# Steps of the gated weights set apart, four more H and L tiles, and the residual on VectorE

## The chip, the cores and the metric

The kernel runs on one core of a Trainium2 chip. The metric is the device time of one execution in microseconds, measured in several runs. One more execution was taken with the hardware profiler; all rows of the trace are from it, and its times count from the first instruction of the span.

## The reference

One encoder block for 256 tokens of width 2048, in float32. A first part (gated spatial mixing, neighbourhood attention, output projection and a LayerNorm) makes `x1`; then a retrieval over 16384 single-neuron experts follows, and a second LayerNorm:

```python
q = (xf @ wq).reshape(T, PEER_HEADS, 2, PEER_QHALF)
s = einsum('thpk,hpnk->thpn', q, subkeys)
top_s, top_i = top_k(s, 16)               # per head and half, then 16 of the 256 sums
gate = softmax(best_s)                    # 8 heads x 16 experts a token
h = einsum('td,tkd->tk', xb, u_tab[ib])   # experts' inputs
w = gb * gelu(h)
y = einsum('tk,tkd->td', w, v_tab[ib])
x = layernorm(alpha * x1 + y)
```

## The kernel before, in words

Every large product runs in three passes of a number split in two: `H` is the operand rounded to the matmul's format (ScalarE, L135), `L` is the rest (VectorE, L136). A *unit* is one 128x512 piece of streamed operand: `emit_split` writes its H and L into tiles of the pool `hlp`, and later the unit's matmuls read them. `hlp` has LOOK + 1 = 4 pairs. `run_units` writes the program in order: for each unit it first emits the splits that may run ahead (at most two in a turn, as long as four pairs or fewer are out), then the unit's matmuls, then what a finished block asks for (`posts`), then one step of each background *lane* (attention, top-k, list making, the residual, the final normalization). Every engine executes its own instructions in that order.

The stages that the change touches:

- *Retrieval.* 64 units of the query weights; top-k runs on VectorE in the background, `VEC_PER_UNIT` = 0.72 us a unit. From here on the new pool of the change exists.
- *Expert products.* All 128 blocks of experts are multiplied densely, four units a block (`stationary_units`: per unit four pairs of matmuls, L224 of 512 columns and L226 of 256). Blocks alternate between two PSUM banks. After a block ScalarE copies one half of the sums (L268), VectorE adds the other (L613), and ScalarE makes the Gelu (L620) and writes it to a table in device memory (L622). SyncE loads the weights into five `raw` tiles of two units each. Lists of the tokens' experts are made meanwhile.
- *Lists ready.* SyncE is given four loads of value blocks `vraw` (L761) and six of table tiles `tb` (L772); the last raw loads stand behind them.
- *Values.* `SEQ` is a list of 109 blocks of 128 value rows: 53 serve both halves of the tokens (24 matmuls) and 56 one half (12). A block has four units (dc 0 to 3, 512 columns each) of three matmuls a half: L235, L236, L237. Its rows come by a gather on GpSimd (L763, five `vraw` tiles), its gates and activations by gathers from the table (L775, four `tb` tiles). `w_split` makes the stationary operand: product of gate and activation (VectorE, L786), its high half (ScalarE, L787), its low half (VectorE, L788), all just before the split of the block's first unit; then it issues the gather for three blocks later.
- *Residual.* After four blocks, `residual` loads `x1` (`x1d`) and the LayerNorm's two rows by GpSimd's queue and makes 16 operations of 128x512 on GpSimd (L1060), six units apart.
- *End.* The three last blocks (LAST) run column part by column part; their H and L tiles are kept, since the second half of the tokens is multiplied after the first while VectorE finishes the first half.

The lines of the splits in the code:

```python
act.activation(H, raw, AF.Copy)
vec.tensor_tensor(L, raw, H.bitcast(F32), op=OP.subtract)
```

Of the kernel before, what the change touches and what calls it, by code (L numbers as in the profile page):

```python
# [31 lines left out]

RAW_BUFS = 5
LOOK = 3

# [25 lines left out]
def tile_encoder_block(ctx: ExitStack, tc: tile.TileContext, a, out):  # L63
# [55 lines left out]
    def emit_split():  # L119
        n = state["split"]  # L120
        if n >= len(units):
            return
        if units[n].early:
            units[n].early()
        kind, r, h = units[n].src
        src = vraws if kind else raws
        raw = src[r][0][:, h * 512:(h + 1) * 512]
        if units[n].dest:
            H, L = units[n].dest()
        else:  # L130
            H = hlp.tile([P, 512], F32R, name="H", tag="H")
            L = hlp.tile([P, 512], F32R, name="L", tag="L")
        if len(H.shape) == 3:
            raw = raw.rearrange("p (k t) -> p k t", t=T)
        act.activation(H, raw, AF.Copy)  # L135
        vec.tensor_tensor(L, raw, H.bitcast(F32), op=OP.subtract)  # L136
        HL[n] = (H, L)
        state["split"] += 1
        src[r][1] -= 1
        if src[r][1] == 0:  # L140
            del src[r]
            if kind:
                emit_values()
            else:
                emit_load()

    credit = {"v": 0.0}

    def step_lanes():
# [28 lines left out]
    def run_units(upto):  # L178
        while state["mm"] < upto:
            n = state["mm"]  # L180
            ahead = 0
            while state["split"] < len(units):
                u = units[state["split"]]
                if state["split"] > n and ahead == 2 or not u.dest and state["out"] > LOOK:
                    break
                state["out"] += not u.dest
                ahead += 1
# [202 lines left out]
    def pause(n):  # L390
        for _ in range(n):
            yield
# [383 lines left out]
                if n == DENSE:  # L776
                    after(i, put[tb] + hput[tb])

    def w_split(n):
        def f():  # L780
            hs = SEQ[n][0]
            s = slice(hs[0], hs[-1] + 1)
            t = tabs.pop(n)
            w = vp.tile([P, 2, 2, P], F32R, name="w", tag="wv", bufs=4)
            p = t[:, s, P:]
            vec.tensor_tensor(p, t[:, s, :P], p, op=OP.mult)  # L786
            act.activation(w[:, 0, s, :], p, AF.Copy)  # L787
            vec.tensor_tensor(w[:, 1, s, :], p, w[:, 0, s, :].bitcast(F32), op=OP.subtract)  # L788
            W[n] = w
            while vst["tab"] < min(n + 4, len(SEQ)) and (SEQ[vst["tab"]][1] < 0 or len(hput[1]) == NKEY):  # L790
                emit_tab()
        return f

    def v_units():
        us = []
        places = [(n, dc) for n in range(len(SEQ) - LAST) for dc in range(4)]
        places += [(n, dc) for dc in range(4) for n in range(len(SEQ) - LAST, len(SEQ))]
        seen = set()
        for n, dc in places:
            hs = SEQ[n][0]  # L800

# [5 lines left out]
            def mm(H, L, n=n, dc=dc, hs=hs):  # L807
# [8 lines left out]
                elif hs == (0, 1):  # L816
                    part(1)

            u = Unit(mm, pre=pre, early=None if n in seen else w_split(n),
                     dest=(lambda n=n, dc=dc: [endp.tile([P, 512], F32R, name="%s%d_%d" % (q, n, dc)) for q in "HL"])  # L820
                     if n >= len(SEQ) - LAST else None,
                     post=(lambda dc=dc: fin["y"](dc)) if n == len(SEQ) - 1 else None)
            u.src = (1, n, dc)
            seen.add(n)
            us.append(u)
        return us


# [157 lines left out]

    up_stack = ExitStack()
    upp = up_stack.enter_context(tc.tile_pool(name="upp", bufs=1))
    gate["g"] = upp.tile([P, 2, PH, TK], F32, name="gate_g")
    gate["i"] = upp.tile([P, 2, PH, TK], U32, name="gate_i")  # L990
    for n, dt in (("tab", U32), ("val", U32)):
# [59 lines left out]
    def residual():  # L1051
# [3 lines left out]
        for tb in range(2):  # L1055
            for c in range(4):
                s = slice(c * 512, (c + 1) * 512)
                for j, op in enumerate((OP.mult, OP.add)):
                    yield from pause(6)
                    pool.tensor_tensor(x1b[:, tb, s], x1b[:, tb, s], gb1[:, j, s], op=op)  # L1060
        ys["y"] = gb1

    def y_ready(dc):
# [136 lines left out]
```

## Time and profile before

| | us |
|---|---|
| median of 3 runs | 1761.7 |
| lowest, highest | 1757.7, 1762.09 |
| the profiled execution | 1757.17 |
| its span, first to last instruction | 1755.4 |
| TensorE matmuls busy | 1695.9 (97%) |
| VectorE busy | 1295.6 (74%) |
| ScalarE busy | 947.7 (54%) |
| GpSimd busy | 858.2 (49%) |
| mean granted clock of TensorE | 0.989 |

PE is TensorE, PEld its weight loads, DVE VectorE, ACT ScalarE, POOL GpSimd, SP SyncE; a small q behind an engine's name is its queue issuing. Busy time says how full an engine is over the whole span. It does not say which engine was waited for at a given moment; windows and timelines of a stretch do.

### The profile page before, as it was taken

How to read it: one execution, taken by the hardware profiler on the slowest of the kernel's cores; microseconds unless marked ns; L12 is line 12 of the kernel's file. 1: busy time of each engine (PE TensorE's matmuls, PEld its weight loads, DVE VectorE, ACT ScalarE, POOL GpSimd, SP SyncE). 2: the span in 40 equal slices, each digit the busy share in tenths (PEclk: the TensorE clock that was granted, in tenths of full speed). 3: DMA queues.
4: the chain of work that ended last, by engine and by line, in shares of the span. 5: the costliest groups of instructions: out<-in, count | busy, mean ns of one | idle time of the engine just before them, and what ended most of it. 6: DMA issues, size and time to landing. Idle time of an engine off the chain costs nothing. (4 is left out here: it accounts for less than half of the span.)

```text
span 1755.4 us, 26746 instructions
## 1 busy us (share of the span) xinstructions
PE 1695.9 (97%) x8544; PEld 1375.6 (78%) x8544; DVE 1295.6 (74%) x2835; ACT 947.7 (54%) x1843; POOL 858.2 (49%) x710
## 2 busy tenths in 40 slices
PE   8999999989999999999999999998989999999995
PEld 7888777878888888888888878887866777777774
DVE  5776665677999998555556888885678777777778
ACT  5655555465555555555555445444545555556553
POOL 0000000000688888888886225771367666666662
PEclk9999999999999999999999999999999999999998
DMA  9998543555678888888888996557687788888881
GB/s 344 379 313 271 190 164 138 193 183 200 175 188 198 202 195 200 220 213 203 214 211 254 359 357 212 189 189 279 240 319 260 262 285 290 291 294 287 285 299 65
DMA packets 201043, 421.66 MB, mean 240 GB/s; under 512 B 53586, under 2 KB 120196, under 8 KB 185796
## 3 DMA queue, kind: packets, MB, share of 16 engines
q1 hardware_dynamic: 98660, 247.50, 41.0%
q0 software_dynamic: 64800, 154.60, 31.1%
q10 hardware_dynamic: 37440, 17.84, 3.8%
q8 instruction: 67, 1.10, 0.3%
q14 instruction: 76, 0.62, 0.1%
HBM read 381.97 MB, written 37.88 MB: 239 GB/s over the span
## 5 line engine op out<-in xcount | busy, mean ns | idle before, releaser
L224 PE MATMUL bank<-xHL,H 128*128 128x512 f32 x2688 | 967.7, 402 | 6.8 <-ACT H L135 6.5
L136 DVE TENSOR_TENSOR L<-raw,H 128x512 fp32r<-128x512 f32 x798 | 545.5, 689 | 304.7 <-ACT H L135 297.1
L226 PE MATMUL bank<-xHL,L 128*128 128x256 f32 x2688 | 759.8, 283 | 5.8 <-DVE L L136 5.0
L135 ACT ACTIVATE H<-raw 128x512 fp32r<-128x512 f32 x798 | 488.2, 628 | 439.7 <-PE bank L224 207.1
L224 PEld LDWEIGHTS bank<-xHL,H 128*128 128x128 f32 x2688 | 506.6, 188 | 129.8 <-ACT H L135 10.4
L226 PEld LDWEIGHTS bank<-xHL,L 128*128 128x128 f32 x2688 | 508.7, 189 | 21.3 <-DVE L L136 19.6
L597 POOL DMA_INDIRECT tab<-gate_g,gate_i x256 | 419.0, 1637 | 133.4 <-issue 75.6
L136 DVE TENSOR_TENSOR L<-vraw,H 128x512 fp32r<-128x512 f32 x436 | 293.4, 717 | 67.5 <-ACT H L135 60.3
L135 ACT ACTIVATE H<-vraw 128x512 fp32r<-128x512 f32 x436 | 248.7, 620 | 64.2 <-PE bank L236 62.8
L235 PE MATMUL bank<-H,w 128*128 128x512 f32 x648 | 260.3, 402 | 11.5 <-ACT H L135 11.4
L237 PE MATMUL bank<-L,w 128*128 128x512 f32 x648 | 264.0, 407 | 3.2 <-DVE L L136 2.9
L236 PE MATMUL bank<-H,w 128*128 128x512 f32 x648 | 258.5, 399 | 2.1 <-DVE w L788 2.1
L775 POOL DMA_INDIRECT tb<-tab,list_tab x154 | 182.2, 1183 | 46.1 <-issue 45.5
L982 POOL DMA_DIRECT2D x1d<-res x1 | 0.5, 547 | 381.3 <-DVE res L952 381.3
L763 POOL DMA_INDIRECT vraw<-in_pv,list_val x105 | 99.5, 948 | 162.7 <-DVE L L136 89.1
L237 PEld LDWEIGHTS bank<-L,w 128*128 128x128 f32 x648 | 122.7, 189 | 53.9 <-DVE L L136 27.2
L235 PEld LDWEIGHTS bank<-H,w 128*128 128x128 f32 x648 | 122.8, 190 | 51.6 <-ACT H L135 26.3
L236 PEld LDWEIGHTS bank<-H,w 128*128 128x128 f32 x648 | 122.8, 190 | 30.4 <-DVE w L788 2.7
L707 POOL TENSOR_SCALAR hotA<-iota,w 128x128 bf16<-128x128 bf16 x124 | 92.9, 760 | 61.6 <-PE bank L718 35.3
L787 ACT ACTIVATE w<-tb 128x128 fp32r<-128x128 f32 (+1 forms) x109 | 39.5, 363 | 145.1 <-DVE tb L786 144.0
L620 ACT ACTIVATE hs<-half 128x256 f32<-128x256 f32 x128 | 52.4, 409 | 88.3 <-DVE half L613 88.2
L788 DVE TENSOR_TENSOR w<-tb,w 128x128 fp32r<-128x128 f32 (+1 forms) x109 | 47.7, 438 | 46.8 <-ACT w L787 46.8
(185 smaller groups left out, 1345.3 us busy)
## 6 DMA issues: line engine op xcount, KB each, us to landing
raw<-in_ut SPq DMA_DIRECT2D x256, 512.0 KB
tab<-zero SPq DMA_DIRECT2D x32, 512.0 KB
raw<-in_wqk SPq DMA_DIRECT2D x32, 512.0 KB
raw<-in_wout SPq DMA_DIRECT2D x32, 512.0 KB
raw<-in_wq SPq DMA_DIRECT2D x32, 512.0 KB
tab<-hs ACTq DMA_DIRECT2D x256, 64.0 KB
gc<-tab POOLq DMA_DIRECT2D x32, 512.0 KB
raw<-in_wu SPq DMA_DIRECT2D x16, 512.0 KB
```

Of the source, the lines that this page charges most:

```text
L135: act.activation(H, raw, AF.Copy)
L136: vec.tensor_tensor(L, raw, H.bitcast(F32), op=OP.subtract)
L224: pe.matmul(ps, lhsT=h, rhs=xs["X"][:, k].rearrange("p j t -> p (j t)"), start=k == 0, stop=False)
L226: pe.matmul(ps[:, T:], lhsT=l, rhs=xs["H"][:, k, :], start=False, stop=k == KD - 1)
L235: pe.matmul(ps, lhsT=h, rhs=H, start=first, stop=False)
L236: pe.matmul(ps, lhsT=l, rhs=H, start=False, stop=False)
L237: pe.matmul(ps, lhsT=h, rhs=L, start=False, stop=last)
L597: i = apart(tb, pool.indirect_dma_start(out=tab[tb].rearrange("e (t o) -> (e t) o", o=1), out_offset=bass.IndirectOffsetOnAxis(ap=gate["i" ...
L620: act.activation(s, held["t"], AF.Gelu)
L707: pool.tensor_scalar(A, iota, row[:, b:b + 1], None, op0=OP.is_equal)
L763: pool.indirect_dma_start(out=t, out_offset=None, in_=a["pv"], in_offset=column(n, "val"))
L775: i = pool.indirect_dma_start(out=t[:, tb, :], out_offset=None, in_=tab[tb], in_offset=column(n, "tab")).ins
```

## The change

Three things change together. (1) From the retrieval on there are eight H and L pairs (`MORE` = 4 in a new pool `more`), and splits may run up to seven units ahead. (2) `w_split` becomes `w_steps`: the product stands three units before the block's first split, the high half one before, the low half at it; the gather of the table tile for three blocks later stays with the low half. (3) The residual's 16 operations are VectorE's, 16 units apart. So that memory suffices, the kept tiles of the end use the five raw tiles first.

```diff
+MORE = 4
@@ emit_split
-            H = hlp.tile([P, 512], F32R, name="H", tag="H")
-            L = hlp.tile([P, 512], F32R, name="L", tag="L")
+            p = hlp
+            if more:
+                p = more["p"] if more["n"] > LOOK else hlp
+                more["n"] = (more["n"] + 1) % (LOOK + 1 + MORE)
+            H = p.tile([P, 512], F32R, name="H", tag="H")
+            L = p.tile([P, 512], F32R, name="L", tag="L")
@@ run_units
-                if state["split"] > n and ahead == 2 or not u.dest and state["out"] > LOOK:
+                if state["split"] > n and ahead == 2 or not u.dest and state["out"] > LOOK + (MORE if more else 0):
@@ w_split becomes w_steps
+    def w_steps(n):
+        hs = SEQ[n][0]
+        s = slice(hs[0], hs[-1] + 1)
+        def product():
+            t = tabs[n]
+            vec.tensor_tensor(t[:, s, P:], t[:, s, :P], t[:, s, P:], op=OP.mult)
+        def high():
+            W[n] = vp.tile([P, 2, 2, P], F32R, name="w", tag="wv", bufs=4)
+            act.activation(W[n][:, 0, s, :], tabs[n][:, s, P:], AF.Copy)
+        def low():
+            vec.tensor_tensor(W[n][:, 1, s, :], tabs.pop(n)[:, s, P:], W[n][:, 0, s, :].bitcast(F32), op=OP.subtract)
             while vst["tab"] < min(n + 4, len(SEQ)) and (SEQ[vst["tab"]][1] < 0 or len(hput[1]) == NKEY):
                 emit_tab()
-        return f
+        return product, high, low
@@ v_units
+        def kept(i):
+            if i < RAW_BUFS:
+                t = rawp.tile([P, 1024], F32R, name="raw", tag="raw")
+                return t[:, :512], t[:, 512:]
+            return [endp.tile([P, 512], F32R, name="%s%d" % (q, i)) for q in "HL"]
...
+            if n not in seen:
+                seen.add(n)
+                for back, f in zip((3, 1, 0), w_steps(n)):
+                    todo[max(len(us) - back, 0)].append(f)
@@ after the first LayerNorm
+    more.update(p=up_stack.enter_context(tc.tile_pool(name="more", bufs=MORE)), n=0)
@@ residual
-                    yield from pause(6)
-                    pool.tensor_tensor(x1b[:, tb, s], x1b[:, tb, s], gb1[:, j, s], op=op)
+                    yield from pause(16)
+                    vec.tensor_tensor(x1b[:, tb, s], x1b[:, tb, s], gb1[:, j, s], op=op)
```

The same work stands in another order on the engines. Line numbers of the changed kernel are higher by 5 to 23 (L135 and L136 become L140 and L141, L786 to L788 become L792, L796 and L799); the numbers behind names count tiles and differ between the two.

VectorE in the values' stage, before: `tb` is a table tile and its product, `w` the low half, `L` the splits.

```order
L786 TENSOR_TENSOR tb_14369<-tb_14369 128x2x128
L788 TENSOR_TENSOR w_14519<-tb_14369,w_14519 128x256
L136 TENSOR_TENSOR L_14526<-vraw_14306,H_14525 128x512
L136 TENSOR_TENSOR L_14533<-vraw_14306,H_14532 128x512
L136 TENSOR_TENSOR L_14541<-vraw_14306,H_14540 128x512
L136 TENSOR_TENSOR L_14548<-vraw_14306,H_14547 128x512
L786 TENSOR_TENSOR tb_14418<-tb_14418 128x128
L788 TENSOR_TENSOR w_14559<-tb_14418,w_14559 128x128
```

The same place on VectorE in the changed kernel:

```order
L799 TENSOR_TENSOR w_14487<-tb_14348,w_14487 128x256
L141 TENSOR_TENSOR L_14508<-vraw_14273,H_14507 128x512
L792 TENSOR_TENSOR tb_14397<-tb_14397 128x128
L141 TENSOR_TENSOR L_14519<-vraw_14273,H_14518 128x512
L141 TENSOR_TENSOR L_14529<-vraw_14273,H_14528 128x512
L141 TENSOR_TENSOR L_14541<-vraw_14273,H_14540 128x512
L799 TENSOR_TENSOR w_14538<-tb_14397,w_14538 128x128
L141 TENSOR_TENSOR L_14554<-vraw_14334,H_14553 128x512
```

The product of the next block (`tb_14397`) now stands after the first split of the block at hand, three splits ahead of its low half.

SyncE where the lists are ready, before: the last value block, six table tiles, then the last raw tiles of the expert weights.

```order
L761 DMA vraw_13931<-in_pv 128x2048
L772 DMA tb_13935<-tab0_96 128x256
L772 DMA tb_13935<-tab1_97 128x256
L772 DMA tb_13938<-tab0_96 128x256
L772 DMA tb_13938<-tab1_97 128x256
L772 DMA tb_13941<-tab0_96 128x256
L772 DMA tb_13941<-tab1_97 128x256
L113 DMA raw_13948<-in_ut 128x1024
L113 DMA raw_13982<-in_ut 128x1024
L113 DMA raw_14008<-in_ut 128x1024
L113 DMA raw_14042<-in_ut 128x1024
```

The same place on SyncE in the changed kernel:

```order
L767 DMA vraw_13954<-in_pv 128x2048
L778 DMA tb_13958<-tab0_96 128x256
L778 DMA tb_13958<-tab1_97 128x256
L778 DMA tb_13961<-tab0_96 128x256
L778 DMA tb_13961<-tab1_97 128x256
L778 DMA tb_13964<-tab0_96 128x256
L778 DMA tb_13964<-tab1_97 128x256
L114 DMA raw_13971<-in_ut 128x1024
L114 DMA raw_14005<-in_ut 128x1024
```

Two raw loads instead of four stand behind the table tiles; the other two were issued before.

ScalarE at the end of the expert products, before: `half` is the copy of a block's half-sums, `hs` the Gelu; `raw_13948` is the first of the raw tiles behind the table tiles.

```order
L135 ACTIVATE H_14064<-raw_13894 128x512
L268 ACTIVATE half_14077<-bank0_14010 128x256
L135 ACTIVATE H_14080<-raw_13948 128x512
L620 ACTIVATE hs_14092<-half_14077 128x256
L622 DMA tab0_96<-hs_14092 128x128
L622 DMA tab1_97<-hs_14092 128x128
L135 ACTIVATE H_14096<-raw_13948 128x512
L135 ACTIVATE H_14108<-raw_13982 128x512
L135 ACTIVATE H_14120<-raw_13982 128x512
L268 ACTIVATE half_14133<-bank1_14068 128x256
```

The same in the changed kernel, where `raw_13971` is the first such tile:

```order
L140 ACTIVATE H_14083<-raw_13917 128x512
L274 ACTIVATE half_14096<-bank0_14031 128x256
L140 ACTIVATE H_14099<-raw_13971 128x512
L626 ACTIVATE hs_14111<-half_14096 128x256
L628 DMA tab0_96<-hs_14111 128x128
L628 DMA tab1_97<-hs_14111 128x128
L140 ACTIVATE H_14115<-raw_13971 128x512
L140 ACTIVATE H_14127<-raw_14005 128x512
L140 ACTIVATE H_14139<-raw_14005 128x512
L274 ACTIVATE half_14152<-bank1_14087 128x256
```

The two pieces read alike, but the splits are those of units eight ahead where they were four ahead: in the changed kernel `H_14139` is the last unit of the last block, and `half_14152` belongs to the last block but two, whose bank the last block needs.

## Rows read from the trace of the kernel before

**Rows 1.** Windows in us; busy time (instructions) by engine, PEclk granted clock, DMA share, GB/s.
```profile
450.00:700.00 250.00, 245.25 (x1367) 208.03 (x1367) 232.77 (x732) 136.57 (x266) 211.92 (x126) 1.00 0.83 195
700.00:950.00 250.00, 249.50 (x1412) 215.96 (x1411) 137.97 (x226) 139.89 (x271) 208.51 (x133) 1.00 0.84 210
950.00:1050.00 100.00, 98.21 (x532) 80.88 (x531) 81.48 (x114) 48.10 (x97) 26.85 (x31) 1.00 1.03 358
...
1200.00:1250.00 50.00, 45.27 (x236) 38.12 (x235) 24.91 (x47) 23.75 (x48) 2.98 (x3) 0.93 0.76 280
1250.00:1400.00 150.00, 139.32 (x553) 103.73 (x552) 117.83 (x180) 76.78 (x151) 103.26 (x94) 0.98 0.77 278
1400.00:1700.00 300.00, 296.12 (x1220) 223.15 (x1219) 224.82 (x423) 178.66 (x352) 188.98 (x174) 1.00 0.83 290
```

**Rows 2.** Timeline, TensorE, first value matmuls: start us, us, instruction [idle before <-releaser].
```profile
1241.80 0.39 PE L235 MATMUL bank<-H,w 128*128 128x512 f32 x1
...
1242.50 0.39 PE L235 MATMUL bank<-H,w 128*128 128x512 f32 x1
```

**Rows 3.** Timelines of SyncE (SPq), ScalarE and TensorE where the lists are ready.
```profile
1211.07 12.14 SPq L772 DMA_DIRECT2D tb<-tab  x6
...
1227.25 0.63 ACT L135 ACTIVATE H<-raw 128x512 fp32r<-128x512 f32 x1 [8.77 <-DMA raw<-in_ut]
1227.78 0.40 ACT L620 ACTIVATE hs<-half 128x256 f32<-128x256 f32 x1
1228.21 0.82 ACTq L622 DMA_DIRECT2D tab<-hs  x2
...
1227.93 0.80 PE L224 MATMUL bank<-xHL,H 128*128 128x512 f32 x1 [4.73 <-ACT H L135]
...
1233.48 0.40 PE L224 MATMUL bank<-xHL,H 128*128 128x512 f32 x1
```

**Rows 4.** Timeline, 1268 to 1294: GpSimd, VectorE, TensorE.
```profile
1268.79 1.01 POOL L775 DMA_INDIRECT tb<-tab,list_tab  x1 [0.30 <-issue]
...
1279.47 1.56 POOL L1060 TENSOR_TENSOR yx<-yx 128x512 f32<-128x512 f32 x1 [5.44 <-DMA yx<-in_ln_g]
...
1282.66 0.43 DVE L786 TENSOR_TENSOR tb<-tb 128x256 f32<-128x256 f32 x1 [2.78 <-DMA tb<-tab,list_tab]
...
1284.11 0.50 PE L235 MATMUL bank<-H,w 128*128 128x512 f32 x1 [2.65 <-ACT H L135]
...
1292.20 2.33 DVE L136 TENSOR_TENSOR L<-vraw,H 128x512 fp32r<-128x512 f32 x1 [0.71 <-ACT H L135]
```

**Rows 5.** Groups by line, 1238 to 1400: count | busy us, mean ns | idle before.
```profile
L136 DVE TENSOR_TENSOR L<-vraw,H 128x512 fp32r<-128x512 f32 x128 | 94.4, 781 | 19.0 <-ACT H L135 16.5 <-DMA vraw<-in_pv,list_val 0.7
...
L1060 POOL TENSOR_TENSOR yx<-yx 128x512 f32<-128x512 f32 x16 | 21.0, 1313 | 5.7 <-DMA yx<-in_ln_g 5.4
```

**Rows 6.** The same groups, 1450 to 1650, with the product.
```profile
L136 DVE TENSOR_TENSOR L<-vraw,H 128x512 fp32r<-128x512 f32 x187 | 121.0, 691 | 30.6 <-ACT H L135 27.9 <-DMA tb<-tab,list_tab 0.7
...
L786 DVE TENSOR_TENSOR tb<-tb 128x256 f32<-128x256 f32 x21 | 8.8, 417 | 0.0
```

**Rows 7.** Timeline of all engines at a block's start, 1505 to 1508.
```profile
1505.99 0.42 ACT L787 ACTIVATE w<-tb 128x256 fp32r<-128x256 f32 x1 [1.09 <-DVE tb L786]
...
1506.44 0.42 DVE L788 TENSOR_TENSOR w<-tb,w 128x256 fp32r<-128x256 f32 x1 [0.48 <-ACT w L787]
...
1507.32 0.40 PE L236 MATMUL bank<-H,w 128*128 128x512 f32 x1
...
1507.71 0.50 PE L237 MATMUL bank<-L,w 128*128 128x512 f32 x1
```

**Rows 8.** Timeline, VectorE in the last part.
```profile
1720.90 6.11 DVE L136 TENSOR_TENSOR L<-vraw,H 128x512 fp32r<-128x512 f32 x10
...
1749.92 0.75 DVE L1047 SCALAR_TENSOR_TENSOR yx<-yx,rs,b2r 128x512 f32<-128x512 f32 x1
```

**Rows 9.** Timeline, GpSimd at the start of the retrieval.
```profile
393.61 0.53 POOL L998 DMA_DIRECT2D subT<-in_subT  x1 [8.14 <-DMA x1d<-res]
```

More of the change, by code (lines that the diff above doesn't have):

```diff
@@ L145, in emit_split @@
                 emit_load()
+    more = {}
     credit = {"v": 0.0}
@@ L777, in emit_tab @@
                     after(i, put[tb] + hput[tb])
[L779 to L789, printed above, removed]
+    def w_steps(n):
[9 more added lines that the diff above has]
+            vec.tensor_tensor(W[n][:, 1, s, :], tabs.pop(n)[:, s, P:], W[n][:, 0, s, :].bitcast(F32), op=OP.subtract)
             while vst["tab"] < min(n + 4, len(SEQ)) and (SEQ[vst["tab"]][1] < 0 or len(hput[1]) == NKEY):
                 emit_tab()
-        return f
+        return product, high, low
     def v_units():
@@ L798, in v_units @@
         seen = set()
+        todo = [[] for _ in places]
+        def kept(i):
[3 more added lines that the diff above has]
+            return [endp.tile([P, 512], F32R, name="%s%d" % (q, i)) for q in "HL"]
         for n, dc in places:
@@ L817, in mm @@
                     part(1)
-            u = Unit(mm, pre=pre, early=None if n in seen else w_split(n),
-                     dest=(lambda n=n, dc=dc: [endp.tile([P, 512], F32R, name="%s%d_%d" % (q, n, dc)) for q in "HL"])
-                     if n >= len(SEQ) - LAST else None,
+            u = Unit(mm, pre=pre, dest=(lambda i=len(us) - len(places) + 4 * LAST: kept(i)) if n >= len(SEQ) - LAST else None,
                      post=(lambda dc=dc: fin["y"](dc)) if n == len(SEQ) - 1 else None)
             u.src = (1, n, dc)
-            seen.add(n)
+            if n not in seen:
+                seen.add(n)
+                for back, f in zip((3, 1, 0), w_steps(n)):
+                    todo[max(len(us) - back, 0)].append(f)
             us.append(u)
+        for u, fs in zip(us, todo):
+            u.early = (lambda fs=fs: [f() for f in fs]) if fs else None
         return us
```

## The prediction

> **What bounds the kernel now.** I read the page first: TensorE is busy for 97% of the span, so time can come only from stretches where it waits or runs slowly. The table of windows [rows 1] shows which those are: the number of matmuls in a stretch, times what one needs when nothing holds it, is taken from the stretch's length. In the values' stage three matmuls start in 0.70 us when undisturbed (1241.80 to 1242.50) [rows 2], so one needs 0.2333 us. From 1250 to 1400 there are 553, or 129.0 us: 21.0 us are lost. From 1400 to 1700 there are 1220, or 284.7: 15.3 lost. In the expert products 1412 matmuls, a pair for each 128 of depth, fill 700 to 950 with TensorE nearly always busy [rows 1], 0.354 us a pair and 1.416 a unit of four; I take that as the floor there. From 950 to 1050, 266 pairs need 94.2 us: 5.8 lost.
>
> The timelines then tell who was late. When the lists are ready, SyncE holds 12.14 us at the table tiles, with raw tiles of the expert weights queued behind it; ScalarE waits 8.77 us for such a tile and TensorE 4.73 us [rows 3]. After the gap the matmuls take longer (0.80 for the first, 0.40 again at 1233.48) and the granted clock of the window is 0.93 [rows 1]; eight pairs take the 5.55 us from 1227.93 to 1233.48 where 2.8 would do. That stall costs 4.73 + 2.7 = 7.4 us. In the values' stage GpSimd waits 5.44 us for the residual's loads, with gathers queued behind it, and TensorE then stands for 2.65 us [rows 4]. After that each of 16 GpSimd operations of 1.31 us holds up VectorE [rows 5]. From 1400 on the residual is over and the loss has another shape: at a block's start ScalarE waits 1.09 us for the product and VectorE 0.48 for the high half, the L tiles come late, and matmuls start up to 0.39 us apart (1507.32, 1507.71) [rows 7].
>
> **The change part by part.**
> *Lists ready.* Eight tiles put the splits four units further, so two of the four raw loads that stood behind the table tiles now stand ahead (SP rows of the change). That is 4 x 1.416 = 5.7 us more work: TensorE, which ran dry at 1223.2, would do so at 1228.9. But ScalarE's copy of the half-sums of the last block but two now stands behind four H splits that need the late tiles (ACT rows), and TensorE's last block needs the bank that this copy frees. From 1227.25: four splits of 0.63, Gelu 0.40 and issue 0.82 [rows 3], an estimated 0.4 for the copy and as much for VectorE's sum (Gelu's time, on a tile of the same shape): about 4.5 us, to 1231.8. A gap of some 2.9 us stays, and I charge its slow restart in full, 2.7. Gain 7.4 - 5.6 = 1.8; ends 0 and 7.4.
>
> *1250 to 1400.* GpSimd's 16 operations go, and its queue never waits for the residual's loads. L splits take 781 ns on average here [rows 5] and 691 later [rows 6]: 128 x 0.09 = 11.5 us of VectorE's time, the lower end. One beside a GpSimd operation takes 2.33 us [rows 4]. The Trainium skill (SBUF, "Who interferes with whom") says that a VectorE instruction with two SBUF inputs and a GpSimd instruction that reads SBUF exclude each other, and the later one waits for all of the other. The 2.33 us agree with that; by it VectorE loses up to 16 x 1.31 = 21.0 us, by the splits' mean 11.5. The upper end is the whole loss, 21.0. I take 19, near it, because the stall at 1284 goes too: the new wait for the residual's loads is VectorE's, ten units later than GpSimd's was. Its loads still crowd the queue: the table gather issued at 1268.79 was waited for until 1282.66 [rows 4], 13.9 us. The product now comes nine units after its gather's issue, not twelve (a unit of this stage takes 1.04 us at the floor: 9.4 us), so VectorE can stand there for 4.5 us with later L splits queued behind it. Seven units ahead, 7.3 us, cover that.
>
> *1400 to 1700.* Product, high and low stand with splits between (DVE rows), so neither engine waits for the other, and a late split has seven units to catch up. At most 15.3 us. VectorE, busy 224.8 of 300 us [rows 1], gets up to 16 x 0.69 = 11.0 more for the residual. Since that is 0.69 (an L split's mean, which has the same shape) in 16 units, it hides; without cover it costs 11.0. Ends 0 and 15.3; I take 13, near the upper, since no bound but these waits shows.
>
> *End.* VectorE runs ten L splits from 1720.90 to 1727.01 and then the normalization to the end; its last instruction starts at 1749.92 [rows 8]. It is the chain there. The three last blocks lose three waits of the 0.48 kind and the splits begin four units (2.8 us) earlier: 1.4 + 2.8, say 4; ends 0 and 6. The tiles kept for the end use the raw tiles, long free: 0.
>
> *Top-k, 450 to 700.* VectorE is busy 232.8 of 250 us [rows 1]: it is the bound. Three more L splits (2.1 us) now precede the half-sum that a new block waits for, one step of background work (0.72) fewer: -1.3, paid once if the rate is VectorE's. Other end: four splits done ahead, +2.8. I take -1, near the queue's order.
>
> *950 to 1050.* The DMA share is 1.03 [rows 1]; four more units of store are filled before the list's loads begin. Ends 0 and 5.8; I take 1.5, as transfers stay the limit.
>
> *New wait at the start.* The first tile of the new pool lies where x1d's source lay, so ScalarE waits there until that write has landed; the load of subT, which already waits for it, was released at 393.61 [rows 9]. ScalarE has the last pieces of the LayerNorm and nine splits before it, so I take 0; each us that the write were late would hold every split behind it.
>
> Sum: 1.8 + 19 + 13 + 4 - 1 + 1.5 = 38.3 us. The profiled execution took 1757.17 us, which gives 1718.9; it lies 4.5 below the median of the runs, 1761.7. I forecast 1720.
>
> **The rivals.**
> *Transfers become the bound of the values' stage.* 290 GB/s at share 0.83 [rows 1] would have to become 306. If the gathers go no faster, or the product waits for its tile in most blocks because the lead is nine units, the 13 us of the steady part don't come: 1733. Against it: 358 GB/s from 950 to 1050, and no product waits for its tile in a steady stretch of before (idle 0.0 ahead of it [rows 6]), though at twelve units' lead. The Trainium skill (SBUF, "A bandwidth-pool intuition that's wrong") gives HBM about 358 GB/s for a core; by that the 306 fit, and the trace reaches the same 358.
> *The store hides all of the first stall*, if the half-sums come in time: 5.6 us more, 1714.
> *The eight tiles do nothing*, since VectorE and ScalarE follow TensorE as closely as before, and only GpSimd's operations count: 1757.2 - 11.5 = 1746.
> *Slower: the half-sum behind eight splits.* If each block from 450 to 700 (1367 matmuls, 8 x 4 a block: 43 blocks) pays the 1.35 us anew, because the H tiles come free so late that VectorE idles, that costs 58 us against 39 gained: 1776. It decides from 29 blocks on. Against it: when VectorE gives the sum of a block it has four H tiles in store, so it need not idle.
>
> **How the numbers follow.** Forecast 1715 to 1728: 0.53; first stall hidden or more, 1700 to 1715: 0.15; transfers or gathers, about 1733: 0.16; only GpSimd, 1746: 0.06; no change: 0.04; slower: 0.06. All ends together reach from 1699 to 1747. The range 1706 to 1738 leaves out part of the second case, the fourth and the last two. A difference under 0.3% cannot be told from no change. Faster 0.90, same 0.04, slower 0.06.
>
> **What would show it.** After: TensorE's matmuls from the first of the values' stage to the last within 460 to 465 us (495.8 now); no GpSimd tensor operation before the end; L splits of 0.7 us throughout, 16 VectorE operations of 0.69 among them. At the lists a gap of 2 to 4 us with a slow restart, ended by a half-sum of VectorE, not by an H split. A wrong step would show as VectorE waiting for table tiles in steady blocks, a TensorE that waits at each block's start in the top-k stretch, or matmuls no closer on average than now after 1400, with gathers late.

## The result and the profile after

| | us |
|---|---|
| before, median of 4 runs | 1761.39 |
| changed kernel, median of 4 runs (lowest, highest) | 1714.76 (1709.34, 1718.76) |
| ratio, 95% interval | 0.974 [0.970, 0.977] |
| the profiled execution of the changed kernel, its span | 1712.3, 1710.4 |
| forecast, range | 1720, 1706 to 1738 |

The changed kernel is 2.6% faster, as forecast in direction and nearly in size. The stretches of its trace come first. In each row stand the window, its length, the busy time of TensorE (with the number of matmuls), of its weight loads, of VectorE, ScalarE and GpSimd, then the granted clock, the DMA share and GB/s.

```profile
450.00:700.00 250.00, 242.08 (x1370) 208.09 (x1369) 233.89 (x734) 136.33 (x267) 210.72 (x126) 1.00 0.85 194
700.00:950.00 250.00, 249.92 (x1435) 218.94 (x1434) 140.97 (x234) 142.18 (x276) 207.34 (x133) 1.00 0.91 215
950.00:1050.00 100.00, 94.73 (x526) 79.97 (x525) 80.66 (x112) 46.94 (x95) 26.94 (x31) 1.00 1.03 352
...
1200.00:1250.00 50.00, 44.73 (x228) 37.91 (x228) 24.97 (x47) 23.15 (x48) 4.44 (x5) 0.93 0.77 273
1250.00:1400.00 150.00, 148.69 (x643) 120.40 (x642) 114.37 (x223) 94.88 (x179) 102.36 (x94) 1.00 0.88 322
1400.00:1650.00 250.00, 250.00 (x1082) 202.79 (x1081) 197.32 (x382) 168.78 (x310) 169.62 (x153) 1.00 0.87 308
```

The number of matmuls in a window tells what was gained: in 1250 to 1400 there are 643 where there were 553, and from 1400 on 1082 in 250 us where there were 1220 in 300 [rows 1]. From 700 to 950 there are 23 more, where the prediction had taken the rate before for a floor. From 1200 to 1250 nothing was gained. 250 us by 1082 is 0.2311 us a matmul; that is the floor of this stage, and the 0.2333 of [rows 2] was 1% too high.

The lists, in the changed kernel: SyncE's queue, ScalarE, VectorE, TensorE (start, duration, what, and in brackets the idle time before and what ended it).

```profile
1209.16 13.52 SPq L778 DMA_DIRECT2D tb<-tab  x6
...
1227.52 0.63 ACT L140 ACTIVATE H<-raw 128x512 fp32r<-128x512 f32 x1 [10.81 <-DMA raw<-in_ut]
...
1230.93 0.36 ACT L274 ACTIVATE half<-bank 128x256 f32<-128x256 f32 x1
...
1231.83 0.42 DVE L619 TENSOR_TENSOR half<-bank,half 128x256 f32<-128x256 f32 x1
...
1226.76 0.28 PE L232 MATMUL bank<-xHL,L 128*128 128x256 f32 x1
1232.31 0.80 PE L230 MATMUL bank<-xHL,H 128*128 128x512 f32 x1 [5.27 <-DVE half L619]
...
...
1240.74 0.39 PE L241 MATMUL bank<-H,w 128*128 128x512 f32 x1
```

SyncE is held at the table tiles, 13.5 us now. The raw tile behind them lets ScalarE go on at 1227.52, where it was 1227.25 [rows 3]. The half copy (1230.93) stands behind four H splits, VectorE's half-sum (1231.83) behind the copy, and TensorE's gap of 5.27 us ends with that half-sum, as the prediction had it; before it ended with an H split.

The place of the residual's loads, on VectorE and TensorE:

```profile
1281.90 0.29 DVE L792 TENSOR_TENSOR tb<-tb 128x128 f32<-128x128 f32 x1 [7.91 <-DMA tb<-tab,list_tab]
...
1282.85 0.50 PE L243 MATMUL bank<-L,w 128*128 128x512 f32 x1 [1.31 <-DVE L L141]
```

VectorE stands 7.91 us at a product whose table tile lands late, behind the residual's loads, with all later L splits queued behind it. TensorE works from what is in store and stops only for the rest.

The groups by line from 1250 to 1400 (count, busy time, mean ns, idle time before):

```profile
L141 DVE TENSOR_TENSOR L<-vraw,H 128x512 fp32r<-128x512 f32 x143 | 93.9, 686 | 14.4 <-ACT H L140 9.6 <-issue 2.1 <-PE bank L241 1.6
...
L792 DVE TENSOR_TENSOR tb<-tb 128x256 f32<-128x256 f32 x17 | 7.1, 420 | 9.4 <-DMA tb<-tab,list_tab 9.4
...
L1083 DVE TENSOR_TENSOR yx<-yx 128x512 f32<-128x512 f32 x8 | 5.6, 698 | 0.0
```

L splits take 686 ns on average where they took 781 [rows 5]. The residual's operations are VectorE's, 698 ns each, eight of them in this window. All of VectorE's idle time before products of two-half blocks (9.4 us) ends with a table tile that comes late, and 12.9 us before those of one-half blocks.

### The profile page after: what moved, and what is told of

The parts are those of the page before. It is cut to its first block, busy times and chain, and to the rows that moved or that the text cites. A ratio compares the mean times of both kernels' runs of the same rounds, so it can differ in the third digit from the quotient of the medians.

```text
span 1710.4 us, 26674 instructions
## 1 busy us (share of the span) xinstructions
PE 1657.8 (97%) x8544; PEld 1379.3 (81%) x8544; DVE 1271.1 (74%) x2851; ACT 961.2 (56%) x1843; POOL 842.4 (49%) x694
## 3 DMA queue, kind: packets, MB, share of 16 engines
q0 software_dynamic: 64800, 154.60, 32.1%
## 5 line engine op out<-in xcount | busy, mean ns | idle before, releaser
L141 DVE TENSOR_TENSOR L<-raw,H 128x512 fp32r<-128x512 f32 x798 | 545.5, 690 | 298.5 <-ACT H L140 278.6
L140 ACT ACTIVATE H<-raw 128x512 fp32r<-128x512 f32 x798 | 486.2, 628 | 432.1 <-PE bank L230 201.7
L141 DVE TENSOR_TENSOR L<-vraw,H 128x512 fp32r<-128x512 f32 x431 | 285.9, 688 | 73.5 <-ACT H L140 58.3
L140 ACT ACTIVATE H<-vraw 128x512 fp32r<-128x512 f32 x431 | 265.6, 628 | 123.8 <-PE bank L242 75.3
L243 PE MATMUL bank<-L,w 128*128 128x512 f32 x638 | 251.0, 393 | 1.3 <-DVE L L141 1.3
L242 PE MATMUL bank<-H,w 128*128 128x512 f32 x638 | 251.4, 394 | 0.0
L241 PE MATMUL bank<-H,w 128*128 128x512 f32 x638 | 250.9, 393 | 0.0
L769 POOL DMA_INDIRECT vraw<-in_pv,list_val x105 | 122.5, 1167 | 138.7 <-DVE L L141 79.6
L781 POOL DMA_INDIRECT tb<-tab,list_tab x154 | 165.8, 1077 | 48.3 <-issue 46.0
L241 PEld LDWEIGHTS bank<-H,w 128*128 128x128 f32 x638 | 119.9, 188 | 28.2
L242 PEld LDWEIGHTS bank<-H,w 128*128 128x128 f32 x638 | 119.7, 188 | 27.6
L274 ACT ACTIVATE half<-bank 128x256 f32<-128x256 f32 x168 | 61.4, 365 | 0.1
L646 POOL DMA_DIRECT2D gc<-tab x32 | 28.4, 887 | 65.7 <-DVE mx L654 58.4
```

Source lines behind the costliest of these rows:

```text
L241: pe.matmul(ps, lhsT=h, rhs=H, start=first, stop=False)
L242: pe.matmul(ps, lhsT=l, rhs=H, start=False, stop=False)
L243: pe.matmul(ps, lhsT=h, rhs=L, start=False, stop=last)
L274: act.activation(t, ps[:, T:], AF.Copy)
L769: pool.indirect_dma_start(out=t, out_offset=None, in_=a["pv"], in_offset=column(n, "val"))
L781: i = pool.indirect_dma_start(out=t[:, tb, :], out_offset=None, in_=tab[tb], in_offset=column(n, "tab")).ins
```

## The experiments

Two theories stood against each other. *By parts:* each part takes away a loss of its own: the residual's move that of 1250 to 1400, tiles and steps together that of the steady part. *By store:* all losses of the values' stage are work that comes late by some microseconds; enough tiles in store cover any of them, wherever it is from.

### One part undone

Residual back on GpSimd:

```diff
-                    yield from pause(16)
-                    vec.tensor_tensor(x1b[:, tb, s], x1b[:, tb, s], gb1[:, j, s], op=op)
+                    yield from pause(6)
+                    pool.tensor_tensor(x1b[:, tb, s], x1b[:, tb, s], gb1[:, j, s], op=op)
```

> The changed kernel with one part undone: the residual's 16 operations are GpSimd's again, six units apart; eight tiles and the three steps stay. Theory (GpSimd's operations hold up VectorE's splits, and its queue of gathers stands behind the residual's loads; a store of seven units cannot make up for VectorE's time): the stretch 1250 to 1400 loses 11.5 to 19 us again, time 1726 to 1734. Rival (the seven units in store would have covered the residual by themselves; what was lost before was slack, not VectorE's time): within 4 us of 1715.

Measured: 1718.55 us (1716.97 to 1719.65), ratio to before 0.977 [0.975, 0.979]: 4 us above the changed kernel, with intervals that overlap. The time is the rival's. That the tiles would have covered the residual by themselves is not shown here, since the steps are there too; the run with the tiles alone (below) shows that they don't.

```profile
1250.00:1400.00 150.00, 145.69 (x620) 114.74 (x619) 117.25 (x198) 81.49 (x165) 116.87 (x103) 1.00 0.84 302
...
L141 DVE TENSOR_TENSOR L<-vraw,H 128x512 fp32r<-128x512 f32 x132 | 94.2, 750 | 3.2 <-ACT H L140 2.4 <-PE bank L243 0.7
...
L792 DVE TENSOR_TENSOR tb<-tb 128x256 f32<-128x256 f32 x15 | 13.8, 923 | 14.2 <-DMA tb<-tab,list_tab 14.2
...
L1083 POOL TENSOR_TENSOR yx<-yx 128x512 f32<-128x512 f32 x16 | 20.8, 1300 | 6.1 <-DMA yx<-in_ln_g 5.8
```

The contention is there: splits take 750 ns where they take 686 without it, 132 x 0.064 = 8.4 us of VectorE's time, and products of two-half blocks take 923 where they take 420, 15 x 0.503 = 7.5 us more. By the rule in the Trainium skill (SBUF — State Buffer, "Who interferes with whom"), that a VectorE instruction with two SBUF inputs and a GpSimd instruction that reads SBUF exclude each other, an upper estimate is 16 x 1.30 = 20.8 us. The trace agrees with it in direction, with 15.9. TensorE loses only 23 matmuls, or 5.3 us: tiles and steps together cover the rest.

Product, high and low half at one place again:

```diff
-                for back, f in zip((3, 1, 0), w_steps(n)):
+                for back, f in zip((0, 0, 0), w_steps(n)):
```

> The changed kernel with one part undone: product, high and low half all at the block's first split again; eight tiles and the residual on VectorE stay. Theory (the steady part from 1400 on lost its time because VectorE needs about 3.3 us for a one-half block of 2.8 us and has nothing in store; with seven units in store the handshake of about 1.5 us a block is absorbed, since VectorE with it needs some 7.9 us in the 8.3 us of a two-half and a one-half block): 1715 to 1720. Rival (the handshake makes VectorE the bound, whatever is in store): most of the 13 us of the steady part and a part of the rest come back, 1728 to 1740.

Measured: 1716.2 us (1711.31 to 1717.69), 0.975 [0.973, 0.977]; not to be told from the changed kernel. The theory holds: the handshake is absorbed.

```profile
1400.00:1650.00 250.00, 250.00 (x1081) 202.83 (x1081) 202.25 (x382) 155.65 (x311) 157.09 (x152) 1.00 0.88 308
...
L799 DVE TENSOR_TENSOR w<-tb,w 128x256 fp32r<-128x256 f32 x28 | 11.9, 426 | 13.6 <-ACT w L796 12.6 <-issue 1.0
L796 ACT ACTIVATE w<-tb 128x256 fp32r<-128x256 f32 x28 | 11.7, 420 | 39.3 <-DVE tb L792 39.3
```

ScalarE waits 39.3 us for products and VectorE 12.6 for high halves in this window (two-half blocks alone), and TensorE makes 1081 matmuls all the same.

Four pairs of tiles:

```diff
-    more.update(p=up_stack.enter_context(tc.tile_pool(name="more", bufs=MORE)), n=0)
```

> The changed kernel with one part undone: four H and L pairs as before; three steps and the residual on VectorE stay. Theory (the store does most in the steady part): 8 to 15 us of the values' stage come back, and pairs in the expert products from 700 to 950 take 0.353 us again in place of 0.348 (6 us if all of it comes from the store): 1726 to 1736. Rival (the steps do it alone; the store is nothing): within 4 us of 1715. The gap at the lists would be about as long either way, released by an H split as before and not by a half-sum.

Measured: 1728.52 us (1722.86 to 1731.51), 0.982 [0.980, 0.985]: 14 us above the changed kernel, in the range of the theory and by the two terms that it named. But the steady part, where it put most of the first, keeps its gain:

```profile
700.00:950.00 250.00, 249.43 (x1411) 215.99 (x1411) 138.93 (x233) 139.89 (x269) 209.13 (x132) 1.00 0.89 211
1250.00:1400.00 150.00, 145.75 (x619) 116.77 (x618) 111.20 (x213) 93.85 (x172) 92.73 (x87) 0.99 0.84 305
1400.00:1650.00 250.00, 250.00 (x1072) 200.75 (x1071) 195.70 (x378) 168.76 (x308) 164.76 (x152) 1.00 0.86 305
...
1285.83 0.67 PE L243 MATMUL bank<-L,w 128*128 128x512 f32 x1 [4.25 <-DVE L L141]
```

The steady part makes 1072 matmuls with four tiles: the steps hold it nearly alone. 5.5 us (24 matmuls) are lost from 1250 to 1400, the stall at the residual's loads above all (TensorE stands 4.25 us there), and 24 matmuls of the expert products from 700 to 950, some 4 us. The rest is not divided here. At the lists TensorE's gap, 4.30 us, ends with an H split again, as expected.

### One part alone

The residual alone is the kernel before with this edit:

```diff
-                    yield from pause(6)
-                    pool.tensor_tensor(x1b[:, tb, s], x1b[:, tb, s], gb1[:, j, s], op=op)
+                    yield from pause(16)
+                    vec.tensor_tensor(x1b[:, tb, s], x1b[:, tb, s], gb1[:, j, s], op=op)
```

> The kernel before with one part of the change alone: the residual's 16 operations on VectorE, 16 units apart. Theory: 1250 to 1400 gains most of its 21 us, less what it loses like the steady part (15.3 us in 300, so 7.7 in 150): about 13 us faster, 1748; the 16 operations spread over 64 blocks cost the steady part up to 11 us without a store to hide them, so 1744 to 1759. Rival (the operations of VectorE cost as much as those of GpSimd did): no change, 1758 to 1763. The rate from 700 to 950 should be that of before, 0.353 us a pair, if it comes from the tiles.

Measured: 1756.04 us (1749.6 to 1757.39), 0.997 [0.996, 0.998]: 5 us faster, in the theory's wide range, less than its 13. The profiled execution took 1751.95 us, 4 us under this median.

The tiles alone are the changed kernel with the first two edits above made together (residual and steps undone).

> The kernel before with one part of the change alone: eight H and L pairs; the steps stay together and the residual is GpSimd's, six units apart. Theory now (what is in store is what counts; the steps and the residual each cost what they cost only where nothing is in store): the values' stage takes 458 to 464 us in place of 495.8, time 1719 to 1726. Rival (two of the three parts are needed, since VectorE with the handshakes and GpSimd's operations has too little time): the stage keeps more than half of its loss, 475 us or more, 1736 or more.

Measured: 1727.03 us (1725.64 to 1730.8), 0.981 [0.979, 0.984]: between the two, as is the values' stage with 466.6 us. The tiles alone make the kernel 33 us faster (the kernel before took 1759.62 in the same rounds); the steady part has all its gain, the residual's stretch less than a third (27 of 90 matmuls).

The steps alone are the changed kernel with the first and the third (residual and tiles undone).

> The kernel before with one part of the change alone: product three units, high half one unit ahead; four pairs of tiles, and the residual is GpSimd's. Theory (steps do by themselves much of what the store does, since with the residual on VectorE and four tiles the stretch from 1300 to 1650 lost only a little; but GpSimd's operations now meet an empty store): the values' stage takes 472 to 480 us, time 1735 to 1744; from 1400 on matmuls as close as in the changed kernel. Rival (the residual's place made the difference, and steps are nothing): 490 us or more, 1755.

Measured: 1734.49 us (1732.1 to 1736.97), 0.985 [0.983, 0.988], just below the theory's range, as is the values' stage with 469.0 us; the rival falls.

The windows of the three (residual alone, tiles alone, steps alone), each from its own trace:

```profile
700.00:950.00 250.00, 249.49 (x1438) 219.45 (x1437) 141.47 (x235) 142.42 (x274) 209.07 (x132) 1.00 0.92 215
1250.00:1400.00 150.00, 145.15 (x594) 110.07 (x593) 108.83 (x203) 83.25 (x163) 88.47 (x84) 0.99 0.83 296
1400.00:1650.00 250.00, 244.73 (x1001) 182.99 (x1000) 189.92 (x354) 146.22 (x288) 154.17 (x143) 1.00 0.83 286
```

```profile
1250.00:1400.00 150.00, 141.54 (x580) 109.70 (x580) 122.55 (x191) 77.69 (x158) 109.42 (x100) 0.98 0.82 290
1400.00:1650.00 250.00, 250.00 (x1081) 202.80 (x1081) 197.89 (x375) 157.39 (x314) 158.53 (x155) 1.00 0.89 312
```

```profile
1250.00:1400.00 150.00, 143.62 (x603) 113.02 (x602) 120.52 (x197) 90.68 (x165) 109.82 (x99) 0.99 0.82 297
1400.00:1650.00 250.00, 250.00 (x1074) 201.09 (x1073) 192.70 (x371) 168.59 (x308) 163.70 (x152) 1.00 0.85 306
```

The tiles alone again, from 1290 to 1390, with VectorE's costliest wait there (us in all, times, longest):

```profile
1290.00:1390.00 100.00, 92.71 (x373) 70.80 (x372) 87.58 (x129) 52.13 (x108) 75.11 (x67) 0.97 0.79 270
...
DVE w L799 <- ACT w L796: 9.4, 22, 0.5
```

The changed kernel makes 434 matmuls there, this one 373. VectorE is busy for 87.58 of 100 us and waits 9.4 for high halves: beside GpSimd's operations it has next to no time left, and a store can't make up for that. From 1400 to 1650 it is busy for 197.89 of 250.

Matmuls from 1250 to 1400 and from 1400 to 1650, and the time from the first to the last value matmul, by the parts a kernel has:

| parts | 1250 to 1400 | 1400 to 1650 | values' stage us | median us |
|---|---|---|---|---|
| none | 553 | 1016 | 495.8 | 1761.4 |
| residual | 594 | 1001 | 488.2 | 1756.0 |
| tiles | 580 | 1081 | 466.6 | 1727.0 |
| steps | 603 | 1074 | 469.0 | 1734.5 |
| tiles, steps | 620 | 1081 | 457.0 | 1718.6 |
| steps, residual | 619 | 1072 | 463.5 | 1728.5 |
| tiles, residual | 639 | 1081 | 453.1 | 1716.2 |
| all three | 643 | 1082 | 451.4 | 1714.8 |

The stage's time is the better measure of a part. The whole time also holds waits that differ from run to run: near 400 TensorE waits 1.5 us for the load of `subT` in the kernel before, 5.3 with tiles and steps, and 4.8 with the steps alone.

In the steady part tiles and steps stand in for each other: either gives nearly all, and both no more. The residual's operations on VectorE cost that part something where neither is there (1001 matmuls for 1016, or 3.5 us), as the prediction said of a lost cover, though less than the 6.2 us that the nine operations there last. From 1250 to 1400 the gains alone are 41, 27 and 50 matmuls, 118 in sum, and 90 together: no part owns this stretch. Over the whole stage they are 7.6, 29.2 and 26.8 us, 63.6 in sum, and 44.4 together. Neither theory holds as it was put: in the steady part the store covers everything, and in the stretch of the residual it covers what is late, but not a VectorE without time left; there steps or the residual's move are needed as well.

### The lists

Table tiles ahead of value blocks:

```diff
-    for _ in range(VBUFS):
-        emit_values()
     for _ in range(3):
         emit_tab()
+    for _ in range(VBUFS):
+        emit_values()
```

> The changed kernel with SyncE's six loads of table tiles ahead of the four loads of value blocks where the lists are ready. Theory (SyncE is held at the table tiles for a write of Gelus to the table that lands late behind the value blocks' data; the raw tiles wait behind it, H splits behind these, the half copy behind four of those, and the half-sum behind that): with the table tiles first SyncE is held under 4 us, the raw tiles land at about 1222 in place of 1228, TensorE's gap shrinks from 5.3 to under 1 us and the slow restart with it, 5 to 8 us faster than the changed kernel: 1707 to 1710. Rival (the data of the value blocks needs the queues until 1220 whatever the order, so the raw tiles land as late as now): gap of 4 us or more, 1713 to 1717.

Measured: 1710.24 us (1709.09 to 1711.7), 0.971 [0.969, 0.973], an interval that overlaps the changed kernel's; the profiled execution took 1711.7 us, the changed kernel's 1712.3. The theory falls, by the trace:

```profile
1204.68 2.77 SPq L778 DMA_DIRECT2D tb<-tab  x6
1207.88 11.10 SPq L767 DMA_DIRECT2D vraw<-in_pv  x4
...
1227.92 0.63 ACT L140 ACTIVATE H<-raw 128x512 fp32r<-128x512 f32 x1 [10.21 <-DMA raw<-in_ut]
```

SyncE is held 11.1 us at the value blocks instead, the raw tile comes at 1227.92, and TensorE's gap is 4.65 us, as the rival has it. The tile's place behind four value blocks sets it, not what is loaded first; behind two, in the next kernel, ScalarE waits half as long for it (5.40 us).

Table tiles, two value blocks, four units of work, then the other three blocks:

```diff
-    for _ in range(VBUFS):
-        emit_values()
     for _ in range(3):
         emit_tab()
+    emit_values()
+    emit_values()
+    run_units(state["mm"] + 4)
+    for _ in range(VBUFS - 2):
+        emit_values()
```

> The changed kernel, at the lists: table tiles first, then two value blocks, then four units of the expert products with what they load, then the other three value blocks. Theory: the last raw tiles land before their splits are due, no gap of TensorE at the lists at all, 7 to 8 us faster than the changed kernel: 1706 to 1709. Rival (the half copy behind four splits alone holds the last block): a gap of 2 us or more released by a half-sum stays, 1711 or more; or the value blocks that come later leave a gap at the start of the values' stage.

Measured: 1711.78 us (1705.52 to 1714.21), 0.971 [0.968, 0.974], no clear gain. The windows, ScalarE at the raw tile, and VectorE and TensorE at the residual's loads:

```profile
1200.00:1250.00 50.00, 49.65 (x268) 41.61 (x268) 27.36 (x51) 25.82 (x53) 4.88 (x5) 1.00 0.84 295
1250.00:1400.00 150.00, 146.63 (x623) 118.53 (x623) 112.45 (x219) 94.67 (x175) 99.46 (x91) 0.98 0.87 317
...
1227.01 0.63 ACT L140 ACTIVATE H<-raw 128x512 fp32r<-128x512 f32 x1 [5.40 <-DMA raw<-in_ut]
...
1281.48 0.29 DVE L792 TENSOR_TENSOR tb<-tb 128x128 f32<-128x128 f32 x1 [9.96 <-DMA tb<-tab,list_tab]
...
1282.43 0.79 PE L243 MATMUL bank<-L,w 128*128 128x512 f32 x1 [3.37 <-DVE L L141]
```

At the lists the theory was right: 268 matmuls from 1200 to 1250 in place of 228 (25 of the 40 are from pairs, half of them the shorter ones), and no gap over 0.25 us. From 1250 to 1400, though, 623 are made in place of 643, and 20 x 0.2311 = 4.6 us are given back: VectorE waits 9.96 us for a table tile, and TensorE 3.37 us.

### Both stalls, and the number of tiles

The residual's loads in 16 parts; before each pair of operations only what the next pair needs:

```diff
-        pool.dma_start(x1b, x1d)
-        pool.dma_start(gb1[:, 0, :], row_bcast(a["ln1_g"], D))
-        pool.dma_start(gb1[:, 1, :], row_bcast(a["ln1_b"], D))
+        def load(i):
+            if i < len(parts):
+                tb, c = parts[i]
+                s = slice(c * 512, (c + 1) * 512)
+                if tb == 0:
+                    pool.dma_start(gb1[:, 0, s], row_bcast(a["ln1_g"][s], 512))
+                    pool.dma_start(gb1[:, 1, s], row_bcast(a["ln1_b"][s], 512))
+                pool.dma_start(x1b[:, tb, s], x1d[:, tb, s])
...
                     yield from pause(16)
+                    if j == 0:
+                        load(i + 1)
                     vec.tensor_tensor(x1b[:, tb, s], x1b[:, tb, s], gb1[:, j, s], op=op)
```

> The changed kernel with the residual's 4 MB of loads in 16 parts of 256 KB, each pair or triple of them ahead of the two operations that need it, in place of three loads at once. Theory (VectorE stands 7.9 us at a block's product because the table gather's data lands behind these loads; the store of seven units runs out, TensorE waits 1.7 us): no wait of VectorE for a table tile over 3 us from 1260 to 1300, no gap of TensorE over 0.6 us after the lists, 1.5 to 2 us faster than the changed kernel, 1713. Rival (the gathers are slow by themselves in this stretch, with 320 GB/s moved): the wait and the gap stay, 1715.

Measured: 1711.02 us (1707.78 to 1715.11), 0.971 [0.969, 0.973]. The time is 4 us below the changed kernel's, with intervals that overlap. In the trace VectorE's longest wait for a table tile from 1260 to 1300 is 2.89 us, and TensorE is busy without a gap after the lists, as the theory said:

```profile
1250.00:1400.00 150.00, 150.00 (x650) 121.75 (x650) 116.77 (x228) 97.77 (x183) 109.47 (x104) 1.00 0.90 320
```

The same with the raw tiles between the value blocks:

> The kernel with raw tiles between the value blocks at the lists (TensorE had no gap there, and one of 3.8 us at 1282 in its place), with the residual's loads in 16 parts. Theory (the 7 us saved at the lists were given back because the store was used up by the residual's loads, which come at the same time as before): without those loads nothing takes them back; the stretch from the first to the last value matmul is 449 to 451 us, as it was 456.4 with the loads at once; 1706. Rival (a store that is short of four or five units at the lists fills again slowly, whatever the loads): a gap of 2 us or more within 60 us of the lists stays, 1710 or more.

Measured: 1703.63 us (1699.63 to 1705.74), 0.966 [0.964, 0.968]: clear of the changed kernel's interval, and some 11 us below its median. This version beats both kernels. Its values' stage takes 450.2 us, as the theory said.

```profile
1200.00:1250.00 50.00, 50.00 (x266) 42.45 (x265) 26.93 (x52) 24.45 (x52) 8.40 (x9) 1.00 0.86 303
1250.00:1400.00 150.00, 150.00 (x649) 121.53 (x649) 117.36 (x232) 95.66 (x188) 113.00 (x105) 1.00 0.91 323
...
1248.76 0.43 DVE L792 TENSOR_TENSOR tb<-tb 128x256 f32<-128x256 f32 x1 [5.90 <-DMA tb<-tab,list_tab]
```

266 matmuls at the lists and 649 after them, all 150 us at the floor of 0.2311. VectorE still waits for table tiles, at most 5.90 us, at 1248.76, and seven units of store cover that: TensorE makes the stage's 1944 matmuls with 0.1 us of idle time.

Six tiles, and ten (the latter from the version with both stalls gone):

```diff
-MORE = 4
+MORE = 2
```

> The changed kernel with six H and L pairs in place of eight (two more than before). Theory (a store has to cover single late splits: the residual's loads of some 8 us, and one-half blocks in which VectorE is slower than TensorE by some 0.5 us): the steady part is as with eight, the stall near 1285 and that at the lists grow by two units, 2.1 and 2.8 us; 1717 to 1721. Rival (each tile counts the same, half of the way to four tiles): 1721 to 1724. If the slow rate of 0.353 us a pair in the expert products comes from too few tiles, it may show here: 1722 to 1728.

Measured: 1718.66 us (1717.12 to 1722.72), 0.976 [0.974, 0.978]: in the theory's range, though the interval overlaps that of eight.

```profile
1250.00:1400.00 150.00, 145.31 (x615) 116.82 (x614) 112.03 (x213) 92.17 (x171) 98.36 (x90) 0.98 0.87 315
...
1283.89 0.79 PE L243 MATMUL bank<-L,w 128*128 128x512 f32 x1 [4.69 <-DVE L L141]
```

The steady part is nearly that of eight tiles (1076 matmuls from 1400 to 1650). From 1250 to 1400 28 matmuls are missing; the stall at the residual's loads (4.69 us) is most of that. It grew by 3.4 us, where the theory had 2.1; the gaps at the lists, 3.93 and 0.94 us, did not grow, where it had 2.8.

```diff
-MORE = 4
+MORE = 6
```

> The kernel with both stalls taken away, and ten H and L pairs in place of eight. Theory (with both stalls gone nothing is left for two more tiles to cover): the same as with eight within 2 us, about 1706. Rival (what is left at the lists and at the top-k stretch is short of tiles): 3 us or more faster, 1703; or slower, since two more splits go ahead of the half-sum in the top-k stretch (450 to 700), 1709.

Measured: 1708.57 us, and inconclusive: the runs go from 1699.8 to 1719.7, 0.968 [0.966, 0.971]. The profiled execution is the slowest of the five, 1719.7 us. In it issuing a gather took GpSimd up to 7.1 us, where one takes 0.93 to 1.5 in the changed kernel. VectorE waited over 6 us for table tiles more than once, and the store ran out:

```profile
1338.71 7.11 POOL L769 DMA_INDIRECT vraw<-in_pv,list_val  x1 [1.26 <-DVE L L141]
...
1332.37 0.29 DVE L792 TENSOR_TENSOR tb<-tb 128x128 f32<-128x128 f32 x1 [6.53 <-DMA tb<-tab,list_tab]
...
1373.73 0.79 PE L243 MATMUL bank<-L,w 128*128 128x512 f32 x1 [2.96 <-DVE L L141]
```

Why issuing is so slow there stays open.

## Why the prediction was right, point by point

*The sum.* 38.3 us were forecast, against the profiled execution's 1757.17. The changed kernel's took 1712.3: 44.9. The values' stage, 1240.74 to the last matmul at 1692.15, takes 451.4 us where 460 to 465 were forecast. That is 44.4 us less than before, nearly all of the gain; TensorE reaches the stage only 1.1 us earlier (1240.74, before 1241.80).

```profile
1692.15 0.39 PE L243 MATMUL bank<-L,w 128*128 128x512 f32 x1
```

*1250 to 1400.* Forecast 19; measured 90 matmuls x 0.2311 = 20.8. The size was right and its owner wrong. The prediction charged the residual's move with it; alone that brings 41 matmuls (9.5 us, under the lower end of 11.5), and taking it back costs 23 (5.3). What failed is the step from "VectorE's splits take 90 ns longer" to "TensorE loses that": it holds only while nothing is in store, and the same change put it there. The splits were also only half of what VectorE lost in the kernel before:

```profile
L788 DVE TENSOR_TENSOR w<-tb,w 128x128 fp32r<-128x128 f32 x15 | 11.6, 777 | 5.7 <-ACT w L787 5.7
```

These low halves take 777 ns from 1250 to 1400 and 292 from 1450 to 1650, 15 x 0.485 = 7.3 us; with splits and the other products and low halves it is some 22 us, about the 21.0 that GpSimd's 16 operations last. VectorE's wait for a table tile was foreseen at up to 4.5 us; 7.91 came, and 1.31 of it reached TensorE.

*1400 on.* Forecast 13, at most 15.3; measured 300 x (1 - (1220/300) / (1082/250)) = 18.1. The term came out short because of the floor: three matmuls whose times are read to 0.01 us gave 0.2333 (0.69 us in place of 0.70 would give 0.2300), and a whole window of a busy TensorE gives 0.2311, 1220 x 0.0022 = 2.7 us less than thought. The prediction gave this term to steps and tiles together; either does by itself (1074 and 1081 matmuls for 1082).

*End.* Forecast 4. What the stage gained besides the two stretches is 495.8 - 451.4 - 20.8 - 18.1 = 5.5, all of it at the end: in the kernel before the last 139 matmuls, 32.1 us at the floor, take the 37.6 us from 1700 on. It is the tiles' gain: from the 144th last value matmul to the last, kernels with eight pairs take 33.1 to 33.9 us, those with four 37.2 to 39.3.

*Lists.* Forecast a gain of 1.8; measured a loss of 0.6 (5.27 + 2.8 against 4.73 + 2.7). The mechanism and the gap's end were right (the half-sum ends at 1232.25, forecast 1231.8). Its start was not: 1228.9 forecast, 1227.04 measured (1226.76 and 0.28). TensorE reached the lists about 2 us earlier (SyncE's table tiles at 1209.16, before 1211.07 [rows 3]), but the raw tile came no earlier. Of two engines that race to the same point the prediction moved one. After the 5.27 us of idle TensorE the restart again was slow: nine pairs at a granted clock of 0.50, or 1.2 GHz, take 5.92 us where 9 x 0.348 = 3.1 would do.

```profile
1232.31:1238.23 5.92, 5.92 (x18) 5.05 (x19) 4.48 (x10) 4.41 (x10) 0.50 (x1) 0.50 0.32 116
```

*700 to 950.* Forecast nothing, since the 1.416 us a unit was taken as the floor; 23 matmuls, or 11.5 pairs x 0.348 = 4.0 us, came. This is the one gain that no term held; some 2 us of it were left at the lists. More on it stands at the end.

*Top-k and 950 to 1050.* Forecast -1 and +1.5; measured three matmuls more (half a microsecond gained) and six fewer (a microsecond lost). Both lie within their ends or a microsecond of them. The slower rival fell: in 250 us TensorE's weight loads waited 11.7 us for half-sums, in 14 places, where that rival wanted 1.35 us in each of 43 blocks, 58 us.

```profile
PEld bank L230 <- DVE half L619: 11.7, 14, 1.9
```

*New wait at the start.* Forecast 0; from 380 to 440 no wait of ScalarE is over 1.3 us, and none is for `x1d`.

*The rivals.* Transfers did not bind: 322 GB/s from 1250 to 1400, under the 358 of [rows 1]. Those are no ceiling in a short stretch: from 1270 to 1280 the kernel before moved 427. That the store hides all of the first stall did not happen, though the time nearly agrees with that case's 1714; a time that fits a rival does not make the rival true. That the eight tiles do nothing is the most wrong of all: they alone bring 33 us, more than the steps (25) or the residual (5).

## What to carry to other kernels

An engine's lost time is the bound engine's loss only while there is nothing in store between them. A store covers work that is late, not an engine that has no time left. Before pricing several losses one by one, ask which of them the same buffer would cover: they overlap, and undoing one part then shows little though it brings much alone. A stall that is taken away gives time only if the next one is not waiting for the same store; here 4.6 us of what was gained at the lists were given back until the residual's loads were spread. And a floor is read from the longest stretch in which the engine is full, not from three instructions.

## What the runs showed of the hardware

The expert products have two rates. From 700 to 950, at a granted clock of 1.00 and with TensorE busy throughout, three of four profiles with four pairs of tiles have 1411 or 1412 matmuls and one has 1438 (the residual alone); all ten profiles with six tiles or more have 1433 to 1437. That is 0.354 or 0.348 us a pair. It is not the store that is waited for: in the kernel before TensorE's matmuls wait 0.5 us in all in this stretch, and the same four tiles show both rates. What decides is open. Issuing a gather, 0.93 to 1.5 us on GpSimd in the changed kernel, took 2.1 to 2.3 us in four places with six tiles, 3.0 to 3.35 in four of the version with both stalls gone, and up to 7.1 with ten tiles.

```profile
1280.04 3.34 POOL L781 DMA_INDIRECT tb<-tab,list_tab  x1 [0.30 <-issue]
```
